# Giving solo projections four PSUM banks in turn in a two-layer hybrid trunk, and moving the norm's broadcast rows

## The chip, the cores and the metric

The kernel runs on one core of a Trainium2 chip. The metric is device microseconds of one execution, the median of several runs. A profile of one execution gives the busy times and waits of the engines: TensorE (PE, matmuls; PEld is its weight load), VectorE (DVE), ScalarE (ACT), GpSimd (POOL) and SyncE (SP, which issues the DMAs).

## The reference

Two layers act on 512 latent tokens `x` and 256 context tokens `y` of width 1024. Each layer norms the tokens, projects them, runs three branches (retention RET, neighbourhood attention NA, grouped-query attention GQA), and merges them under sigmoid gates:

```
hx = rms_norm(x, norm_w) * (1.0 + scale_x) + shift_x
rq, rk, rv, rg, nq, nk, nv, ng, gq, gk, gv, gg, mg = split_cols(hx @ w_in)
...
m = (g_ret * (ret_o @ w_ret_o) + g_na * (na_o @ w_na_o) + g_gqa * (gqa_o @ w_gqa_o))
x = x + gate_x * (m @ w_out)
```

Layer 1 updates `x` alone; a last `rms_norm` gives the output.

## The kernel before

Tokens lie in the free dimension, 768 in layer 0 (512 latent, 256 context), and 512 for most of layer 1. Every fp32 product is made of three fp32r matmuls (`mm3`, lines 278 to 280: high times high, high times low, low times high), so each weight block is split into `whi` (ACT, L262) and `wlo` (POOL, L264). One projection of a 128-wide column block over 512 tokens is a group of 24 matmuls into one PSUM bank, then an "evacuation", in which ACT and DVE read that bank and write SBUF. A projection with tokens in the partitions (`g_proj_tok`, lines 310 to 312) is three groups of 48 matmuls of 256 columns.

PSUM has eight banks. `bank(tag)` hands out tiles from four rings: two tiles of `pj`, two of `s`, three of `pt`, one of `pv`. A tile of a ring may be written when the tile that last held the same bank has been read by all its readers, so in a ring of two a group waits for the evacuation of the group before the last. Projections use `pj`; attention scores, the context rows' outputs (L477), the transposes of the GQA values (`tr`, L784), and the norm's broadcast rows (`bcast_mm`, L387) use `s`.

PE's order is that of the program text, by hand: `run(units)` emits projections with nothing between them ("alone"), `window(steps, units)` mixes attention steps with projections. `defer(us, fn)` puts off a piece of work until the projections emitted since have a given cost, and it then lands between two matmuls of whatever group is running. The orders of DVE and ACT are set by a list scheduler when the program is built, and then fixed.

Places that the text below speaks of:
- After the start phase (which holds four banks for `u_q(0)` and `u_k(0)` of NA at once: the latter's context part in `pj`, its latent part in `pv`, both parts of `u_q(0)` in `s`), `runs(na.u_v(0))` follows: three groups of L310.
- The GQA opening: `runs(gqa.u_k(), gqa.u_v(), gqa.u_q(0))`. The evacuation of `u_v` copies to `sg` (ACT, L779), and its transposes `tr` come 1.5 us of projections later, four for the latent part, two for the context part; each is read by one `gv` cast on ACT (L788) and one `gv` subtraction on DVE (L789). The keys meanwhile go through a long DVE chain that ends in `gk` (`k_fin`, L767 to L770).
- The retention heads: `run(u_qk(h,"q"), u_qk(h,"k"), ...)` before each head's window, evacuated by `ql` and `kl` (L974) on DVE.
- `finish`: the merges of the last branch, the output projection `g_out`, and `norm_part`, whose broadcast row is L387.

Of the kernel before, what the change touches and what calls it, by code (L numbers as in the profile page):

```python
# [39 lines left out]
def trunk_kernel(ctx: ExitStack, tc: tile.TileContext, xt, wcol, wv, adaw, wbr, wout, nabias, vecs,  # L40
# [3 lines left out]
    def tap(name, ap, where):  # L44
        if taps and name in taps:
            nc.sync.dma_start(out=taps[name][where], in_=ap)
# [12 lines left out]
    def bank(tag):  # L59
        return pp.tile([128, 512], F32, tag=tag, name=tag, bufs=PSB[tag])  # L60
# [3 lines left out]

    mm = nc.tensor.matmul
    env = {}


    clock = [0.0]
# [9 lines left out]
    def due(force=False):  # L79
        while waiting:  # L80
            w = min(waiting, key=lambda x: x[0])
            if not force and w[0] > clock[0]:
                return
            waiting.remove(w)
            w[2]()
# [19 lines left out]
            return c  # L105

    def run(units):
        for u in units:
            while u.step() is not None:
                pass  # L110

    NEED = 1.0
    def window(steps, units, lead=0.0, keep=0.0):
# [31 lines left out]
        if not keep:  # L145
            run(units)
# [121 lines left out]
    def getw(src):  # L268
        while len(ready) < 2 and stream:
            _load()  # L270
        s, parts = ready.pop(0)
        assert s is src, "weight stream order"
        while len(ready) < 1 and stream:
            _load()
        return parts

    def mm3(ps, sh, sl, mh, ml, start, stop):
        mm(ps, lhsT=sh, rhs=mh, start=start, stop=False)  # L278
        mm(ps, lhsT=sh, rhs=ml, start=False, stop=False)  # L279
        mm(ps, lhsT=sl, rhs=mh, start=False, stop=stop)  # L280
# [4 lines left out]
    def wk(parts, k, nk=4, width=128):  # L285
        hi, lo = parts[k // nk]
        c = slice((k % nk) * width, (k % nk) * width + width)
        return hi[:, c], lo[:, c]

    def g_proj(w, groups, evac):  # L290
        for o, n in groups:
            ps = bank("pj")
            for k in range(KT):
                sh, sl = wk(w, k)
                mh, ml = hx[k]
                mm3(ps[:, :n], sh, sl, mh[:, o:o + n], ml[:, o:o + n], k == 0, k == KT - 1)
                if k == KT - 1:
                    evac(ps[:, :n], o, n)
                yield 3 * n * NS

    def g_proj_tok(wa, wb, evac):
        for tp in range(3):
            ps = bank("pj")
            for i in range(2):
                tok = slice((2 * tp + i) * 128, (2 * tp + i) * 128 + 128)
                for k in range(KT):
                    hi, lo = wk(wa if k < 4 else wb, k % 4, 2, 256)
                    sh, sl = hx[k]
                    o = ps[:, i * 256:i * 256 + 256]
                    mm(o, lhsT=sh[:, tok], rhs=hi, start=(k == 0), stop=False)  # L310
                    mm(o, lhsT=sh[:, tok], rhs=lo, start=False, stop=False)  # L311
                    mm(o, lhsT=sl[:, tok], rhs=hi, start=False, stop=(k == KT - 1))  # L312
                    if i == 1 and k == KT - 1:
                        evac(ps, tp)
                    yield 3 * 256 * NS
# [4 lines left out]
    def u_proj(src, groups, evac):  # L320
        return Unit(sum(n for _, n in groups) * 24 * NS, [src], lambda ws: g_proj(ws[0], groups, evac), evac)
# [46 lines left out]
    def sumsq(acc, x, first, c, npool, bufs=2):  # L368
        n = c.stop - c.start
        if first:  # L370
            nc.scalar.activation(acc[:, c], x[:, c], AF.Square)
        else:
            sq = npool.tile([128, n], F32, tag="sq", name="sq", bufs=bufs)
            nc.scalar.activation(sq, x[:, c], AF.Square)
            nc.vector.tensor_tensor(acc[:, c], acc[:, c], sq, op=ALU.add)

    def stat_mm(acc, o, n):
        ss = bank("pt")
        for i in range(n // 128):
            mm(ss[:, i:i + 1], lhsT=acc[:, o + 128 * i:o + 128 * i + 128], rhs=ones, start=True, stop=True)  # L380
        return ss

    def bcast_mm(r, o, n, tag="s"):
        bc = bank(tag)
        for i in range(n // 128):
            tb = o // 128 + i
            mm(bc[:, 128 * i:128 * i + 128], lhsT=r[:, tb:tb + 1].to_broadcast([128, 128]), rhs=ident,  # L387
               start=True, stop=True)
        return bc
# [687 lines left out]
    def u_merge(l, b, d, g, m, getpool):  # L1077
        gq = G_ALL if l == 0 else G_LAT
        nq = NT if l == 0 else NX
        src = [ap_wcol[l][CT_MG + 8 * b + d]]  # L1080
        if d % 2 == 0:
            src.append(ap_wbr[l][b][d // 2])

        def gen(ws):
            if d % 2 == 0:
                wbr_now[0] = ws[1]
            t = getpool().tile([128, nq], F32, tag="mt", name="mt", bufs=1)

            def ev(ps, o, n):
                nc.scalar.activation(t[:, o:o + n], ps, AF.Tanh, scale=0.5)  # L1090
            yield from g_proj(ws[0], gq, ev)
            hi, lo = wbr_now[0][d % 2]
            if len(g) < 4:
                due(True)
            for o, n in gq:
                ps = bank("pj")
                for k in range(4):
                    c = slice(k * 128, k * 128 + 128)
                    gh, gl = g[k]
                    mm3(ps[:, :n], hi[:, c], lo[:, c], gh[:, o:o + n], gl[:, o:o + n], k == 0, k == 3)  # L1100
                    if k == 3:
                        c = slice(o, o + n)
                        if b == BR_NA:
                            nc.vector.scalar_tensor_tensor(m[d][:, c], t[:, c], 1.0, ps[:, :n], op0=ALU.add, op1=ALU.mult)
                        else:
                            nc.vector.scalar_tensor_tensor(t[:, c], t[:, c], 1.0, ps[:, :n], op0=ALU.add, op1=ALU.mult)  # L1106
                            nc.vector.tensor_tensor(m[d][:, c], m[d][:, c], t[:, c], op=ALU.add)
                    yield 3 * n * NS
        return Unit(nq * 36 * NS, src, gen)

    wbr_now = [None]
# [141 lines left out]
    def finish(l, m, mtp):  # L1253
# [27 lines left out]
        def g_out(half, o, n):  # L1281
            for d in range(KT):
                w = getw(ap_wout[l][half][d])
                xo = op.tile([128, 512], F32, tag="xo", name="xo", bufs=2)
                nc.sync.dma_start(out=xo[:, :n], in_=xsrc[:, d * st + o:d * st + o + n])
                ps = bank("pj")
                for k in range(KT):
                    sh, sl = wk(w, k)
                    mh, ml = mhl[k]
                    mm3(ps[:, :n], sh, sl, mh[:, o:o + n], ml[:, o:o + n], k == 0, k == KT - 1)  # L1290
                    if k == KT - 1:
                        s = 1 if o >= NX else 0
                        with tc.high_priority(HP):
                            nc.vector.scalar_tensor_tensor(xn[d][:, o:o + n], ps[:, :n], cG[l][:, d, s:s + 1], xo[:, :n],
                                                           op0=ALU.mult, op1=ALU.add)
                            sumsq(accs["t"], xn[d], d == 0, slice(o, o + n), op)
                        if l == 0 and o == 0:
                            nc.sync.dma_start(out=env["xsave"][:, d * NX:(d + 1) * NX], in_=xn[d][:, :NX])
                        tap(f"x{l}", xn[d][:, o:o + n], (d, slice(None), slice(o, o + n)))
                    yield 3 * n * NS  # L1300
# [6 lines left out]
        def norm_part(o, n, use, go, w1=3.0, w2=4.0):  # L1307

            r = cp.tile([128, 6], F32, tag="rstd", name="rstd", bufs=2)

            def one():
                ss = stat_mm(accs["t"], o, n)
                nb = n // 128
                rsqrt(r[:, o // 128:o // 128 + nb], ss[:, :nb], nb, 1.0 / D, EPS)
                go(w2, two)

            def two():
                bc = bcast_mm(r, o, n)
                for k in range(KT):
                    use(k, bc[:, :n], o, n)  # L1320
            go(w1, one)
# [10 lines left out]
        def hx_part(k, bcv, o, n):  # L1332
            make_hx(1, k, xn[k], bcv, o, n, npool)
        use = hx_part if l == 0 else out_part
        parts = ((0, 512), (512, 256)) if l == 0 else ((0, 256), (256, 256))
        if l == 0:
            new_hx()
        for half, (o, n) in enumerate(parts):
# [9 lines left out]
            else:  # L1348
                due(True)
                norm_part(o, n, use, lambda wait, fn: fn())  # L1350
        env["lo_dve"] = False
        cm.__exit__(None, None, None)
        mtp["cm"].__exit__(None, None, None)
        env["gcm"].__exit__(None, None, None)
# [129 lines left out]
```

## Time and profile before

| | |
|---|---|
| median of 3 runs | 1745.47 us (1740.78 to 1746.36) |
| profiled execution | 1744.02 us |
| its span, first to last instruction | 1742.2 us |
| mean granted TensorE clock | 0.993 |
| PE busy | 1665.9 us (96%) |
| DVE busy | 1056.7 us (61%) |
| ACT, POOL busy | 796.8 us (46%), 556.4 us (32%) |

PE's busy time is the sum of modelled matmul spans and touches 96% of the span; the other engines are well below. A row of a timeline gives start, duration, engine, line, operation, output and inputs, shapes, the count of equal instructions in a row, and in brackets the idle time of that engine just before and what ended it.

### The profile page before, as it was taken

How to read it: one execution, taken by the hardware profiler on the slowest of the kernel's cores; microseconds unless marked ns; L12 is line 12 of the kernel's file. 1: busy time of each engine (PE TensorE's matmuls, PEld its weight loads, DVE VectorE, ACT ScalarE, POOL GpSimd, SP SyncE). 2: the span in 40 equal slices, each digit the busy share in tenths (PEclk: the TensorE clock that was granted, in tenths of full speed). 3: DMA queues.
4: the chain of work that ended last, by engine and by line, in shares of the span. 5: the costliest groups of instructions: out<-in, count | busy, mean ns of one | idle time of the engine just before them, and what ended most of it. 6: DMA issues, size and time to landing. Idle time of an engine off the chain costs nothing. (4 is left out here: it accounts for less than half of the span.)

```text
span 1742.2 us, 26141 instructions
## 1 busy us (share of the span) xinstructions
PE 1665.9 (96%) x9940; PEld 1439.5 (83%) x9940; DVE 1056.7 (61%) x2201; ACT 796.8 (46%) x1570; POOL 556.4 (32%) x486
## 2 busy tenths in 40 slices
PE   6899999999999999999999999999999999999997
PEld 4778888888899889888887889877787897887786
DVE  6666567666654655565324766668677646555456
ACT  4455564555553443443223445654555544344342
POOL 1433332233233222322222343423333333243432
PEclk9999999999999999999999999999999999999998
DMA  8211111111111121214536521311111121122245
GB/s 317 80 51 56 58 49 49 37 49 37 37 60 49 49 61 37 63 50 157 203 133 206 171 97 47 99 49 61 49 58 52 60 73 61 61 76 70 91 136 160
DMA packets 43053, 146.38 MB, mean 84 GB/s; under 512 B 4912, under 2 KB 10160, under 8 KB 39856
## 3 DMA queue, kind: packets, MB, share of 16 engines
q1 hardware_dynamic: 42928, 144.72, 25.0%
q8 instruction: 78, 1.28, 0.3%
q14 instruction: 47, 0.39, 0.1%
HBM read 140.51 MB, written 4.19 MB: 83 GB/s over the span
## 5 line engine op out<-in xcount | busy, mean ns | idle before, releaser
L264 POOL TENSOR_TENSOR wlo<-raw,whi 128x512 fp32r<-128x512 f32 x345 | 457.3, 1330 | 972.3 <-ACT whi L262 923.6
L278 PE MATMUL pj<-hxh,whi 128*128 128x512 f32 (+1 forms) x1448 | 527.7, 364 | 9.8 <-DVE ql L974 3.9
L279 PE MATMUL pj<-hxl,whi 128*128 128x512 f32 (+1 forms) x1448 | 510.3, 352 | 1.1 <-DVE hxl L404 1.1
L280 PE MATMUL pj<-hxh,wlo 128*128 128x512 f32 (+1 forms) x1448 | 509.7, 352 | 0.0
L262 ACT CAST whi<-raw 128x512 fp32r<-128x512 f32 x376 | 231.4, 618 | 293.2 <-PE pj L279 214.8
L278 PEld LDWEIGHTS pj<-hxh,whi 128*128 128x128 f32 x1448 | 274.2, 189 | 43.1 <-DVE ql L974 5.8
L280 PEld LDWEIGHTS pj<-hxh,wlo 128*128 128x128 f32 x1448 | 273.9, 189 | 39.0
L279 PEld LDWEIGHTS pj<-hxl,whi 128*128 128x128 f32 x1448 | 274.9, 190 | 28.1 <-DVE hxl L404 2.2
L439 DVE TENSOR_TENSOR pl<-pt,ph 128x512 fp32r<-128x512 f32 (+2 forms) x208 | 126.7, 625 | 52.9 <-ACT ph L438 50.7
L278 PE MATMUL pj<-gat,whi 128*128 128x512 f32 (+1 forms) x416 | 144.6, 348 | 2.6 <-ACT gat L917 2.0
L279 PE MATMUL pj<-gat,whi 128*128 128x512 f32 (+1 forms) x416 | 142.4, 342 | 0.6 <-DVE gat L1271 0.3
L280 PE MATMUL pj<-gat,wlo 128*128 128x512 f32 (+1 forms) x416 | 142.0, 341 | 0.0
L438 ACT CAST ph<-pt 128x512 fp32r<-128x512 f32 (+2 forms) x208 | 107.6, 533 | 69.4 <-PE pt L624 29.4
L310 PE MATMUL pj<-whi,hxh 128*128 128x256 f32 x384 | 110.5, 288 | 3.1 <-DVE kz L427 2.3
L312 PE MATMUL pj<-whi,hxl 128*128 128x256 f32 x384 | 109.4, 285 | 0.0
L311 PE MATMUL pj<-wlo,hxh 128*128 128x256 f32 x384 | 109.4, 285 | 0.0
L278 PEld LDWEIGHTS pj<-gat,whi 128*128 128x128 f32 x416 | 79.2, 190 | 11.9 <-ACT gat L917 2.5
L862 ACT ACTIVATE p<-p,nm,rq 128x768 f32<-128x768 f32 x64 | 65.4, 1024 | 46.7 <-DVE nm L860 46.1
L280 PEld LDWEIGHTS pj<-gat,wlo 128*128 128x128 f32 x416 | 79.0, 190 | 9.4
L279 PEld LDWEIGHTS pj<-gat,whi 128*128 128x128 f32 x416 | 79.1, 190 | 8.9 <-DVE gat L1271 0.5
L853 DVE TENSOR_SCALAR_CACHE_REDUCE p<-s 128x384 f32<-128x384 f32 x128 | 69.0, 554 | 28.0 <-PE s L852 26.7
L1106 DVE SCALAR_TENSOR_TENSOR mt<-mt,pj 128x512 f32<-128x512 f32 (+1 forms) x48 | 28.6, 596 | 91.9 <-PE pj L280 91.3
(265 smaller groups left out, 2957.6 us busy)
## 6 DMA issues: line engine op xcount, KB each, us to landing
raw<-in_wcol_dram SPq DMA_DIRECT2D x116, 512.0 KB, 3.5
araw<-in_adaw_dram SPq DMA_DIRECT2D x24, 1024.0 KB, 6.4
raw<-in_wout_dram SPq DMA_DIRECT2D x32, 512.0 KB, 3.5
raw<-in_wbr_dram SPq DMA_DIRECT2D x24, 512.0 KB, 3.5
raw<-in_wv_dram SPq DMA_DIRECT2D x16, 512.0 KB, 3.5
bias<-in_nabias_dram SPq DMA_DIRECT2D x16, 384.0 KB, 3.1
x<-in_xt_dram SPq DMA_DIRECT2D x8, 384.0 KB, 6.0
xo<-in_xt_dram SPq DMA_DIRECT2D x8, 256.0 KB, 3.7
```

Of the source, the lines that this page charges most:

```text
L262: nc.scalar.copy(hi, raw[:, c])
L264: lo_eng.tensor_tensor(lo, raw[:, c], f(hi), op=ALU.subtract)
L278: mm(ps, lhsT=sh, rhs=mh, start=start, stop=False)
L279: mm(ps, lhsT=sh, rhs=ml, start=False, stop=False)
L280: mm(ps, lhsT=sl, rhs=mh, start=False, stop=stop)
L310: mm(o, lhsT=sh[:, tok], rhs=hi, start=(k == 0), stop=False)
L311: mm(o, lhsT=sh[:, tok], rhs=lo, start=False, stop=False)
L312: mm(o, lhsT=sl[:, tok], rhs=hi, start=False, stop=(k == KT - 1))
L438: nc.scalar.copy(ph[:, :n], pt[:, :n])
L439: nc.vector.tensor_tensor(pl[:, :n], pt[:, :n], f(ph[:, :n]), op=ALU.subtract)
L853: nc.vector.tensor_scalar(P[:, jj, kk], s[:, :384], 1.0, -3.0e38, op0=ALU.mult, op1=ALU.max, accum_out=mx[:, i:i + 1])
L862: nc.scalar.activation(P[:, a], P[:, a], AF.Exp, bias=nm[:, a:a + 1], scale=rqe[:, 2 * hf + a:2 * hf + a + 1], accum_out=sm[:, a:a + 1])
```

## The change

A function `pbank()` hands out the bank of a projection group. While the flag `alone` is set (inside `run`, and in `finish` from the output projection on) it gives `s` and `pj` in turn; otherwise `pj`. The turn goes on over the whole program: it is toggled at every projection group, alone or not. The broadcast rows in `finish` go to `pv` (first part) and `pt` (second part) in place of `s`. The numbers of banks per ring stay as they are.

```diff
+    turn = [0]
+    def pbank():
+        turn[0] ^= 1
+        return bank("s" if env.get("alone") and turn[0] else "pj")
...
     def run(units):
+        env["alone"] = True
         for u in units:
             while u.step() is not None:
                 pass
+        env["alone"] = False
...
     def g_proj(w, groups, evac):
         for o, n in groups:
-            ps = bank("pj")
+            ps = pbank()
...
     def g_proj_tok(wa, wb, evac):
         for tp in range(3):
-            ps = bank("pj")
+            ps = pbank()
...
             for o, n in gq:
-                ps = bank("pj")
+                ps = pbank()
...
-                ps = bank("pj")
+                ps = pbank()
                 for k in range(KT):
                     sh, sl = wk(w, k)
                     mh, ml = mhl[k]
...
             def two():
-                bc = bcast_mm(r, o, n)
+                bc = bcast_mm(r, o, n, "pv" if o == 0 else "pt")
...
         use = hx_part if l == 0 else out_part
+        env["alone"] = True
...
-        env["lo_dve"] = False
+        env["lo_dve"] = env["alone"] = False
```

PE's order of work, and those of POOL and SP, are the same; banks differ, and with them what PE waits for. DVE and ACT differ in a few places only. Lines of the change stand 6 to 9 lower down than those of before; the numbers after tile names are the same in both programs.

The first place is PE at the first group of `u_v(0)` in layer 0 (tile 621), just after the start phase. Before:

```order
L278 MATMUL pj_263<-hxh_179,whi_147 128x256
L279 MATMUL pj_263<-hxl_180,whi_147 128x256
L280 MATMUL pj_263<-hxh_179,wlo_148 128x256
L310 MATMUL pj_621<-whi_252,hxh_165 128x256
L311 MATMUL pj_621<-wlo_253,hxh_165 128x256 [waits Pool_49]
L312 MATMUL pj_621<-whi_252,hxl_166 128x256
```

Now:

```order
L286 MATMUL pj_263<-hxh_179,whi_147 128x256
L287 MATMUL pj_263<-hxl_180,whi_147 128x256
L288 MATMUL pj_263<-hxh_179,wlo_148 128x256
L318 MATMUL s_621<-whi_252,hxh_165 128x256 [waits DVE_49,PE_49]
L319 MATMUL s_621<-wlo_253,hxh_165 128x256 [waits Pool_49]
L320 MATMUL s_621<-whi_252,hxl_166 128x256
```

Tile 621 moved from the free `pj` bank to the first `s` bank, which holds the latent part of `u_q(0)` (tile 260), and waits for DVE. The second group of `u_v(0)` takes the free `pj` bank and waits for nothing, the third the other `s` bank.

The second place is PE in the GQA opening of layer 0: the first group of `u_q(0)` (tile 2969), with the second transposes `tr` (tile 2976) inside it. Before:

```order
L278 MATMUL pj_2969<-hxh_167,whi_2856 128x512
L279 MATMUL pj_2969<-hxl_168,whi_2856 128x512
L280 MATMUL pj_2969<-hxh_167,wlo_2857 128x512
L784 MATMUL s_2976<-ident_90,sg_2918 128x128 [waits Activation_49]
L784 MATMUL s_2976<-ident_90,sg_2918 128x128
```

Now:

```order
L286 MATMUL s_2969<-hxh_167,whi_2856 128x512
L287 MATMUL s_2969<-hxl_168,whi_2856 128x512
L288 MATMUL s_2969<-hxh_167,wlo_2857 128x512
L792 MATMUL s_2976<-ident_90,sg_2918 128x128 [waits DVE_49]
L792 MATMUL s_2976<-ident_90,sg_2918 128x128
```

The projection now stands in the `s` ring between the first transposes (tile 2930) and the second (2976), so 2976 falls on the bank of 2930 and waits for DVE to have read it; before it waited for ACT's copy `sg` alone. Layer 1 reads the same with tiles 12457 and 12503. On DVE, at the same place, before (`gk` are the halves of the keys):

```order
L789 TENSOR_TENSOR gv_2760<-s_2930,gv_2760 128x2x64
L789 TENSOR_TENSOR gv_2760<-s_2976,gv_2760 128x2x64
L768 TENSOR_TENSOR gk20_2758<-kr_2796,gk10_2756 64x768
L769 CAST gk10_2756<-gk10_2756 64x768
L770 CAST gk20_2758<-gk20_2758 64x768
L768 TENSOR_TENSOR gk21_2759<-kr_2796,gk11_2757 64x768
L769 CAST gk11_2757<-gk11_2757 64x768
L770 CAST gk21_2759<-gk21_2759 64x768
L789 TENSOR_TENSOR gv_2760<-s_2930,gv_2760 128x2x64
L789 TENSOR_TENSOR gv_2760<-s_2976,gv_2760 128x2x64
```

Now:

```order
L797 TENSOR_TENSOR gv_2760<-s_2930,gv_2760 128x2x64
L776 TENSOR_TENSOR gk20_2758<-kr_2796,gk10_2756 64x768
L777 CAST gk10_2756<-gk10_2756 64x768
L778 CAST gk20_2758<-gk20_2758 64x768
L776 TENSOR_TENSOR gk21_2759<-kr_2796,gk11_2757 64x768
L777 CAST gk11_2757<-gk11_2757 64x768
L778 CAST gk21_2759<-gk21_2759 64x768
L797 TENSOR_TENSOR gv_2760<-s_2930,gv_2760 128x2x64 x3
L797 TENSOR_TENSOR gv_2760<-s_2976,gv_2760 128x2x64 x2
```

Three of the four readers of tile 2930 stand behind the six instructions on the keys. On ACT, in layer 1, the casts of the weights that stood ahead of and among the `gk` and `gv` casts stand behind them: before,

```order
L788 CAST gv_12287<-s_12503 128x2x64
L262 CAST whi_12539<-raw_12533 128x512
L767 CAST gk10_12283<-kr_12323 64x768
L767 CAST gk11_12284<-kr_12323 64x768
L788 CAST gv_12287<-s_12457 128x2x64
L788 CAST gv_12287<-s_12503 128x2x64
L262 CAST whi_12545<-raw_12543 128x512
```

and now

```order
L775 CAST gk10_12283<-kr_12323 64x768
L775 CAST gk11_12284<-kr_12323 64x768
L796 CAST gv_12287<-s_12457 128x2x64 x3
L796 CAST gv_12287<-s_12503 128x2x64 x2
L270 CAST whi_12539<-raw_12533 128x512
L270 CAST whi_12545<-raw_12543 128x512
```

The weights of the next projection are now cast only after the readers of 12503, and so POOL's `wlo` of them too.

The third place is PE in a retention head of layer 1, where the latent part of `u_qk(1,"k")` (tile 15165) gives way to its context part (15194); the query before them is tile 15126 in `pj`, before as now. Before:

```order
L278 MATMUL pj_15165<-hxh_9584,whi_15122 128x512
L279 MATMUL pj_15165<-hxl_9585,whi_15122 128x512
L280 MATMUL pj_15165<-hxh_9584,wlo_15123 128x512
L278 MATMUL pj_15194<-hxh_9570,whi_15118 128x256 [waits DVE_49]
L279 MATMUL pj_15194<-hxl_9571,whi_15118 128x256
```

Now:

```order
L286 MATMUL s_15165<-hxh_9584,whi_15122 128x512
L287 MATMUL s_15165<-hxl_9585,whi_15122 128x512
L288 MATMUL s_15165<-hxh_9584,wlo_15123 128x512
L286 MATMUL pj_15194<-hxh_9570,whi_15118 128x256 [waits DVE_49]
L287 MATMUL pj_15194<-hxl_9571,whi_15118 128x256
```

Before, 15194 stood on the bank of the query 15126; now 15165 has left the ring, so 15194 stands on the bank of the merge group ahead of the query, and the next `pj` group on that of the query. In layer 0 the second and third head begin with `pj` again, the fourth head and `finish` with `s`.

## Rows read from the trace of the kernel before

**Rows 1.** The page: busy us, share of the span and instructions of each engine.

```profile
PE 1665.9 (96%) x9940; PEld 1439.5 (83%) x9940; DVE 1056.7 (61%) x2201; ACT 796.8 (46%) x1570; POOL 556.4 (32%) x486
```

**Rows 2.** Waits of PE: waiter, releaser: us in total, times, longest.

```profile
PE pj L278 <- DVE ql L974: 3.9, 6, 0.9
PE pj L310 <- DVE kz L427: 2.3, 1, 2.3
PE pj L278 <- DVE mt L1106: 2.0, 4, 0.5
...
PE pj L278 <- DVE kl L974: 1.2, 2, 0.8
...
PE pj L310 <- DVE kl L974: 0.8, 1, 0.8
PE pj L278 <- DVE kz L427: 0.7, 1, 0.7
```

**Rows 3.** Timeline of PE, second retention head of layer 1.

```profile
1462.28 0.38 PE L278 MATMUL pj<-hxh,whi 128*128 128x256 f32 x1 [0.92 <-DVE ql L974]
...
1466.18 0.50 PE L278 MATMUL pj<-hxh,whi 128*128 128x512 f32 x1 [0.78 <-DVE kl L974]
...
1468.36 0.39 PE L278 MATMUL s<-qh,kh 128*128 128x512 f32 x1
```

**Rows 4.** Timeline of DVE, same place.

```profile
1465.45 0.68 DVE L974 SCALAR_TENSOR_TENSOR kl<-pj,kh 128x512 fp32r<-128x512 f32 x1
```

**Rows 5.** Timeline of PE, first and second group of u_v(0), layer 0.

```profile
55.61 0.28 PE L310 MATMUL pj<-whi,hxh 128*128 128x256 f32 x1
...
63.86 0.36 PE L310 MATMUL pj<-whi,hxh 128*128 128x256 f32 x1 [2.34 <-DVE kz L427]
```

**Rows 6.** Timeline of DVE, same place.

```profile
60.17 1.04 DVE L427 SCALAR_TENSOR_TENSOR q<-s,q 64x512 fp32r<-64x512 f32 x2
```

**Rows 7.** Timeline of PE, second transposes of the GQA opening, layer 0.

```profile
269.90 0.44 PE L784 MATMUL s<-ident,sg 128*128 128x128 f32 x2 [0.75 <-ACT sg L779]
```

**Rows 8.** Timeline of DVE, same place.

```profile
272.48 0.68 DVE L707 TENSOR_TENSOR kr<-kr,sh 128x512 f32<-128x512 f32 x1
...
274.06 0.95 DVE L768 TENSOR_TENSOR gk<-kr,gk 64x768 fp32r<-64x768 f32 x1 [0.50 <-ACT gk L767]
...
278.14 0.49 DVE L789 TENSOR_TENSOR gv<-s,gv 128x128 fp32r<-128x128 f32 x2
```

**Rows 9.** Timeline of ACT, same place.

```profile
274.91 0.43 ACT L788 CAST gv<-s 128x128 fp32r<-128x128 f32 x2
```

**Rows 10.** Timeline of PE, GQA opening of layer 1.

```profile
1194.02 0.44 PE L784 MATMUL s<-ident,sg 128*128 128x128 f32 x2 [0.74 <-ACT sg L779]
...
1201.75 0.66 PE L725 MATMUL pt<-ident,gsq 128*128 128x128 f32 x4 [1.14 <-ACT gsq L719]
...
1212.19 0.41 PE L851 MATMUL s<-gk,q 128*128 128x384 f32 x1 [0.91 <-DVE q L427]
```

**Rows 11.** Timeline of DVE, same place.

```profile
1196.60 1.77 DVE L707 TENSOR_TENSOR kr<-kr,sh 128x512 f32<-128x512 f32 x1
...
1201.31 2.05 DVE L768 TENSOR_TENSOR gk<-kr,gk 64x768 fp32r<-64x768 f32 x1
...
1204.46 0.49 DVE L789 TENSOR_TENSOR gv<-s,gv 128x128 fp32r<-128x128 f32 x2
```

**Rows 12.** Timeline of POOL, same place.

```profile
1201.28 1.27 POOL L264 TENSOR_TENSOR wlo<-raw,whi 128x512 fp32r<-128x512 f32 x1 [3.45 <-ACT whi L262]
```

**Rows 13.** Timeline of PE at the end of the last retention window.

```profile
1617.51 0.51 PE L278 MATMUL pj<-gat,whi 128*128 128x512 f32 x1 [2.04 <-ACT gat L917]
```

**Rows 14.** Stretches: length; busy us (instructions) of PE, PEld, DVE, ACT, POOL; granted clock; DMA.

```profile
64.00:68.00 4.00, 4.00 (x35) 4.00 (x36) 0.88 (x3) 0.37 (x1) 0.00 (x0) 1.00 0.02 4
...
1618.80:1622.20 3.40, 3.40 (x10) 2.62 (x9) 2.47 (x3) 1.24 (x2) 1.27 (x1) 0.51 0.10 14
1622.20:1626.00 3.80, 3.80 (x18) 3.16 (x17) 0.52 (x1) 0.73 (x2) 1.29 (x1) 0.99 0.34 125
```

## The prediction

> **What bounds the kernel now.** The page comes first: PE is busy for 96% of the span and DVE for 61% [rows 1]. A change that moves no matmul can only give back, or add, time in which PE stands still, so the view to read next is the one of PE's waits. There the waits that two `pj` banks make are those of a projection (L278, L310) for a DVE evacuation: `ql` 3.9 us in six waits, `kl` 1.2 and 0.8 in three, `mt` 2.0 in four, `kz` 2.3 and 0.7 in one each, 10.9 us in all [rows 2]. That is about the most the change can win, 0.6% of the span. One instance shows the pattern: in the second head of layer 1 the context part of the key projection waits 0.92 us for `ql`, and the next group 0.78 for `kl` [rows 3]. Third, since a wait can move as well as vanish, I followed each tile of the changed order to the tile that held its bank before, and looked up in the timelines of DVE and ACT when that one is read out. Three tiles come out late, and they decide the sign; at the other changed places the bank has been read out before PE comes.
>
> **What the change gives back.** All six waits for `ql` go, since the tile in front of them left the `pj` ring; so do the three for `kl`. Of the four for `mt` two stay: the second and third head of layer 0 still begin on `pj` behind the merges; two go, 1.0 us. The `kz` wait before the first NA window of layer 1 (0.7) goes. Sum 3.9 + 2.0 + 1.0 + 0.7 = 7.6 us in twelve waits [rows 2]. The idle time understates each: a matmul of 512 columns is shown for 0.39 us [rows 3] while their starts are 0.21 us apart (18 in 3.80 us [rows 14]), so a wait costs about 0.17 more than its bracket, 2.0 us over twelve: 9.6. Some comes back as a wait for data. In layer 1's second head the scores stand at 1468.36 [rows 3] and would come two waits and overlaps, 2.0 us, earlier, at 1466.3; the key they need is done at 1465.45 + 0.68 = 1466.13 [rows 4], so almost all is kept there. I take off 0.8 for narrower places, and keep **8.8 us** (bounds 7.0 and 9.6).
>
> **What it adds: `u_v(0)` of layer 0.** Its first group starts at 55.61 in a free `pj` bank and its second at 63.86 after 2.34 us of waiting [rows 5], so a group takes 63.86 - 55.61 - 2.34 = 5.9 us at most. Now the first group stands on the bank of `u_q(0)`, whose last reader is the first of the pair `q` that starts at 60.17 [rows 6]. The pair's 1.04 us covers 512 and 256 columns, so the first part ends near 60.8 and PE starts near 61.0. The second group, which now has a free bank, then starts near 66.7 in place of 63.86: **+2.9 us**. The 2.3 us for `kz` in rows 2 is thereby replaced, not won.
>
> **The GQA opening, layer 0.** This is the dearest term. The second transposes stand at 269.90 [rows 7] and now need the bank of the first, whose four `gv` readers on DVE are in the new order one ahead of the key instructions and three behind. The keys still start at 274.06, when ACT's cast lets them [rows 8], and end where the `gv` pair now stands, at 278.14 [rows 8]. Two `gv` take 0.49, so three end near 278.9; ACT's casts for them are done long before, at 274.91 and after [rows 9]. PE starts near 279.0 rather than 269.90: **+9.1 us**. Nothing covers it: behind the transposes in PE's queue stand the rest of `u_q(0)`, the first merge and the window, and the queries that the window's scores need come out of that very projection. The key chain doesn't wait for PE.
>
> **The GQA opening, layer 1.** The same transposes stand at 1194.02 [rows 10], the `gv` pair at 1204.46 [rows 11]; three `gv` later it would be 1205.2, a stall of 11.3 us. But two steps of that chain are long here: `kr` 1.77 and one `gk` 2.05 [rows 11], where layer 0 took 0.68 and 0.95 [rows 8]. The long `gk` starts beside a POOL `wlo` of 1.27 us at 1201.28 [rows 12]. In the new ACT order the weight casts that feed such `wlo` stand behind the `gv` casts, so POOL has nothing to do there; if both steps shrink to layer 0's size the chain ends 2.1 to 2.2 us sooner. I take 9.2 (bounds 9.1 and 11.3), because the order removes the overlap. On SBUF — State Buffer, section Who interferes with whom, the Trainium skill says that a VectorE instruction with two SBUF inputs contends with a GpSimd instruction that reads SBUF. The trace agrees, 2.05 against 0.95 us; were it not the cause, the time would be 2.1 us more. Two data waits later in this stage, 1.14 for `gsq` and 0.91 for `q` [rows 10], exist because ACT and DVE are still busy with the keys; after the stall they aren't, so these go, with their overlaps -2.3. Net **+6.9 us**.
>
> **The clock.** After a wait of 2.04 us at 1617.51 [rows 13] PE ran 3.4 us at a granted clock of 0.51, the level of 1.2 GHz: 10 matmuls there, against 18 in the 3.80 us that follow at 0.99 [rows 14], so 1.3 us were lost. After the 2.34 us of rows 5 it stayed at 1.00 [rows 14]. Three stalls of 5 to 9 us should each cost such a stretch: 3 x 1.3 = **+3.9 us** (bounds 0, as after rows 5, and 10.2, where each restart has two such stretches at half pace, 3.4 us lost). The Trainium skill's TensorE: Matmul & The Clock Gate, Part 1, says that the array drops from 2.4 to 1.2 GHz after idling and comes back after sustained activity; by that rule all three stalls pay, as I have it, and the trace's one stretch above agrees.
>
> **The broadcast rows.** Four matmul groups change bank. At each, PE waits for `rstd` on DVE, not for a bank, and nothing else is in `pv` or late in `pt` there: 0.
>
> **Sum.** 2.9 + 9.1 + 6.9 + 3.9 - 8.8 = +14.0 us on the profiled execution's 1744.02: **1758 us**, or 0.8% slower. That execution stands 1.5 us below the median of the three runs, which differ by 5.6 among themselves; a change within 0.3% (5.2 us) can hardly be told from none here.
>
> **Rivals.** (1) The stalls come, the clock holds: 1754 us, 0.12. For it speaks the stretch after rows 5, against it that after rows 13. (2) The stalls come dear: layer 1 keeps its long steps (+2.1), the half-clock stretches are longer or two each: 1764 to 1768 us, 0.13. (3) The other side: the wait for the first transposes' bank costs nothing, because the `gv` readers finish before PE arrives. This decides at one place, DVE in the GQA opening: if the three `gv` were done before 269.90, 9.1 + 9.2 us and their clock would fall away, leaving 2.9 + 1.3 - 8.8 = -4.6 (there the 2.3 of relief has no cause), 1739 us, faster by 0.3%. Against it: their order is fixed, behind instructions that can't start before 274.06; it needs a bank assignment other than the one I read. 0.07. (4) The change does nothing that can be measured, because PE's waits for `ql` and `kl` come back one for one as waits for data and the stalls are about half what I have, being met by PE's slack elsewhere: 1749, 0.06. PE's 96% leave little slack.
>
> The likeliest, 1758, has 0.62 and its own range 1755 to 1762. The range for 8 in 10 reaches to (1) and into (2): 1750 to 1766, with the spread of the runs. Slower by over 0.3% takes the likeliest, (1) and (2): 0.87; same 0.07, faster 0.06.
>
> **What the next profile should show.** Right: PE's waits name a transpose into `s` (now L792) for `gv` with some 18 us in two; a wait of about 5 us for `q` ahead of L318; no wait of a projection for `ql` or `kl`, and two for `mt`; the granted clock at half after each of the three. Wrong if the transposes wait for ACT alone, or if the retention heads keep their pairs of waits. The sum is off by the clock if the stretches after the stalls show 1.00.

## The result, and the profile after

The changed kernel took 1764.68 us (median of four runs, 1764.03 to 1766.47) against 1745.91 for the kernel before beside it: ratio 1.0119, 95% interval 1.0107 to 1.0131, some 20.8 us (the two medians alone differ by 18.8). The forecast was 1758, or 0.8% slower, with 1755 to 1762 as the range of its likeliest case and 1750 to 1766 as the wide one: sign and mechanism came out, the size did not. The profiled execution took 1766.47 us, the longest of the four, span 1764.7, mean granted clock 0.981.

Of PE's waits in the changed kernel these bear on the argument (lines 262 to 1294 of before stand 8 lower here); the columns are those of [rows 2].

```profile
PE s L792 <- DVE gv L797: 21.1, 2, 10.5
...
PE s L318 <- DVE q L435: 5.2, 1, 5.2
...
PE pv L395 <- DVE rstd L219: 3.2, 1, 3.2
...
PE pj L286 <- DVE mt L1114: 1.0, 2, 0.5
...
PE s L319 <- POOL wlo L272: 0.7, 1, 0.7
```

All waits for `ql`, `kl` and `kz` of [rows 2] are gone and two of the four for `mt` are left, as forecast. In their place stand one wait of 5.2 us and two of 10.5. The timeline of PE shows where, first at `u_v(0)` (before: [rows 5]), then at the second transposes of the two layers (before: [rows 7, 10]).

```profile
60.89 0.55 PE L318 MATMUL s<-whi,hxh 128*128 128x256 f32 x1 [5.19 <-DVE q L435]
...
286.07 0.69 PE L792 MATMUL s<-ident,sg 128*128 128x128 f32 x2 [10.54 <-DVE gv L797]
286.41 0.78 PE L286 MATMUL s<-hxh,whi 128*128 128x512 f32 x1
286.99 0.63 PE L287 MATMUL s<-hxl,whi 128*128 128x512 f32 x1
...
1217.58 0.69 PE L792 MATMUL s<-ident,sg 128*128 128x128 f32 x2 [10.54 <-DVE gv L797]
```

The matmuls behind the stall show 0.63 us where the same form shows 0.39 at full clock. What PE waits for stands on DVE (answers to [rows 8]):

```profile
279.42 0.28 DVE L797 TENSOR_TENSOR gv<-s,gv 128x128 fp32r<-128x128 f32 x1
280.40 0.95 DVE L776 TENSOR_TENSOR gk<-kr,gk 64x768 fp32r<-64x768 f32 x1 [0.70 <-ACT gk L775]
...
283.90 0.55 DVE L778 CAST gk<-gk 64x768 fp32r<-64x768 f32 x1
284.48 0.29 DVE L797 TENSOR_TENSOR gv<-s,gv 128x128 fp32r<-128x128 f32 x1
285.10 0.29 DVE L797 TENSOR_TENSOR gv<-s,gv 128x128 fp32r<-128x128 f32 x1 [0.33 <-ACT gv L796]
285.73 0.29 DVE L797 TENSOR_TENSOR gv<-s,gv 128x128 fp32r<-128x128 f32 x1 [0.33 <-ACT gv L796]
```

and on ACT (answers to [rows 9]):

```profile
281.24 0.27 ACT L796 CAST gv<-s 128x128 fp32r<-128x128 f32 x1
284.80 0.27 ACT L796 CAST gv<-s 128x128 fp32r<-128x128 f32 x1 [3.30 <-DVE gv L797]
285.43 0.27 ACT L796 CAST gv<-s 128x128 fp32r<-128x128 f32 x1 [0.36 <-DVE gv L797]
```

One `gv` stands ahead of the keys and three behind, as read from the order. But the three don't run back to back: each cast on ACT waits for the subtraction before it on DVE, and each subtraction for its cast, 0.62 us a pair where the forecast had 0.25.

The stretches behind the stalls, with the busy time of PE alone, then the granted clock (before: [rows 14]):

```profile
60.00:64.00 4.00, 3.11 (x14) 0.50 0.01 2
64.00:68.00 4.00, 4.00 (x29) 0.79 0.00 0
94.00:98.00 4.00, 2.69 (x8) 0.80 0.42 131
98.00:102.00 4.00, 4.00 (x22) 0.77 0.00 0
286.00:292.00 6.00, 5.93 (x17) 0.58 0.00 0
1217.00:1223.00 6.00, 5.42 (x14) 0.51 0.00 0
```

0.50 is the 1.2 GHz level. It holds for 4.6 to 5.2 us of PE's work behind each of the three stalls, and for 3.4 us more at 96 us, where PE's waits are those of before (0.74 and 0.99 us) and the clock of the kernel before was at 1.00.

How much later the same matmul starts after the change, followed through the two profiled executions, gives the ledger:

| Place (start before, us) | Step | Later by, us |
|---|---|---|
| 63.86, second group of `u_v(0)` | wait for `q` 2.85 net, half clock 2.1 | 5.0 |
| 93.63 | half clock at 96 us | 6.4 |
| 269.90, second transposes, layer 0 | wait for `gv` 9.8 | 16.2 |
| 276.78 | half clock 2.3 | 18.4 |
| 1035.98 | retention of layer 0 and the norm, -5.1 | 13.3 |
| 1194.02, second transposes, layer 1 | wait for `gv` 9.9, small drifts 0.4 | 23.6 |
| 1196.83 | half clock 2.4 | 25.9 |
| 1201.75 | wait for `gsq` gone, -1.3 | 24.7 |
| 1244.54 | waits for `q` and `p` shorter, new wait for `m`, together -0.2; longer half clock 1.0 | 25.5 |
| 1577.20 | retention of layer 1, -5.4 | 20.1 |
| end | last norm: `rstd` and half clock 2.3 | 22.5 |

### The profile page after: what moved, and what is told of

It reads as the page before. It is cut to its first block, busy times and chain, and to the rows that moved or that the text cites. A ratio compares the mean times of both kernels' runs of the same rounds, so it can differ in the third digit from the quotient of the medians.

```text
span 1764.7 us, 26125 instructions
## 1 busy us (share of the span) xinstructions
PE 1672.6 (95%) x9940; PEld 1448.3 (82%) x9940; DVE 1059.3 (60%) x2201; ACT 797.8 (45%) x1570; POOL 556.9 (32%) x486
## 5 line engine op out<-in xcount | busy, mean ns | idle before, releaser
L286 PE MATMUL pj<-hxh,whi 128*128 128x512 f32 (+1 forms) x1136 | 407.5, 359 | 1.1 <-DVE mt L1114 1.0
L288 PE MATMUL pj<-hxh,wlo 128*128 128x512 f32 (+1 forms) x1136 | 392.6, 346 | 0.0
L287 PE MATMUL pj<-hxl,whi 128*128 128x512 f32 (+1 forms) x1136 | 392.6, 346 | 0.0
L286 PE MATMUL s<-hxh,whi 128*128 128x512 f32 (+1 forms) x328 | 127.5, 389 | 1.8 <-ACT hxh L411 1.8
L287 PE MATMUL s<-hxl,whi 128*128 128x512 f32 (+1 forms) x328 | 125.6, 383 | 2.9 <-DVE hxl L412 2.9
L288 PE MATMUL s<-hxh,wlo 128*128 128x512 f32 (+1 forms) x328 | 124.4, 379 | 0.0
L286 PE MATMUL pj<-gat,whi 128*128 128x512 f32 (+1 forms) x312 | 109.5, 351 | 2.0 <-ACT gat L925 2.0
L287 PE MATMUL pj<-gat,whi 128*128 128x512 f32 (+1 forms) x312 | 107.3, 344 | 0.2 <-DVE gat L926 0.2
L286 PEld LDWEIGHTS s<-hxh,whi 128*128 128x128 f32 x328 | 63.5, 194 | 18.6 <-ACT hxh L411 3.4
L287 PEld LDWEIGHTS s<-hxl,whi 128*128 128x128 f32 x328 | 63.5, 194 | 15.9 <-DVE hxl L412 5.6
L286 PEld LDWEIGHTS pj<-gat,whi 128*128 128x128 f32 x312 | 59.9, 192 | 8.8 <-ACT gat L925 2.5
```

## Experiments

**The dear place undone.** The opening of GQA takes its own two banks in both layers again, the rest stays as changed.

```
-    def run(units):
-        env["alone"] = True
+    def run(units, alone=True):
+        env["alone"] = alone
...
-        runs(gqa.u_k(), gqa.u_v(), gqa.u_q(0))
+        plan.append(("run", [gqa.u_k(), gqa.u_v(), gqa.u_q(0)], False))
```

> The changed kernel with one thing undone: in the opening of GQA, in both layers, the three projections take only their own two banks again. Theory A (the two stalls of 10.5 us before the second transposes, and the half-clock stretches behind them, carry the loss): the changed kernel's trace grew by 9.8 + 2.2 us and 9.9 + 2.4 us against the one before at these two places, and gained 2.1 us of later waits there, so 1764.7 - 24.3 + 2.1 = about 1742 us, a little under the kernel before, and no wait of a transpose for gv. Rival B (the stalls cost what was forecast, and the rest of the overshoot lies elsewhere, in the finish, the broadcast rows or a clock that is low for another reason): 1764.7 - 18 + 2 = about 1748 us, above the kernel before. Rival C (the stalls are covered by slack later in the stage): over 1755 us.

Measured: 1741.01 us, ratio to before 0.9988 (0.9979 to 0.9997). Theory A, within a microsecond: no transpose waits for `gv`, and the change without this place is no longer a loss. The place costs 1.19 + 0.12 = 1.31%, 22.9 us.

**The second place undone too.**

```
-            runs(na.u_v(0))
+            plan.append(("run", [na.u_v(0)], False))
```

> The kernel of the first run of this set, with the first NA value projection of layer 0 on its own two banks as well. Theory A: its 5.2-us wait for q and the slow clock behind it go, 6.35 us by the traces at 93 us, so 1742 - 6.4 = about 1736 us, 0.6% under the kernel before: what is left of the change is the twelve waits given back, 8.8 us forecast. Rival B (the twelve waits come back as waits for data, so that the gain of the retention heads is small): 1742 to 1746 us, no different from the kernel before.

Measured: 1735.78 us, 0.9953 (0.9938 to 0.9968). Theory A again: `u_v(0)` cost 0.35%, 6.1 us (5.2 by the medians), and what is left of the change gains 0.47%, 8.2 us, beside the 8.8 forecast. The wait for `kz` of [rows 5] is back, and no projection waits for `ql` or `kl`; here and in the run before, the first merge of layer 0 waits 1.0 us for a `gv` reader.

```profile
PE pj L318 <- DVE kz L435: 2.3, 1, 2.3
```

**Each loss alone, on the kernel before.** First only the opening of GQA in four banks, then only `u_v(0)`; the diff gives the kernel before `pbank` and a flag that is set for these runs alone.

```
-        runs(gqa.u_k(), gqa.u_v(), gqa.u_q(0))
+        plan.append(("run", [gqa.u_k(), gqa.u_v(), gqa.u_q(0)], True))
```

> The kernel before with one part of the change alone: only the opening of GQA takes the four banks in turn, the broadcast rows stay where they were. Theory A: 9.8 + 2.2 us in layer 0 and 9.9 + 2.4 - 2.1 in layer 1, so before + 22 = about 1768 us, slower than the whole change, since nothing is given back. Rival B (the clock costs 1.3 us at each stall): before + 9.8 + 1.3 + 9.9 + 1.3 - 2.1 = about 1766. Rival C (the stalls make the loss only together with the other banks' use): under 1755 us.

Measured: 1766.04 us, 1.0121 (1.0108 to 1.0134), 21.1 us: between A's 22.2 and B's 20.6, nearer to B by the time, and the interval of 2.3 us each way parts it from neither. C falls.

```
-            runs(na.u_v(0))
+            plan.append(("run", [na.u_v(0)], True))
```

> The kernel before with one part of the change alone: only the first NA value projection of layer 0 takes the four banks in turn. Theory A: a wait of 5.2 us for q in place of 2.3 us for kz, +2.9 us, and a half-clock stretch behind it, +2.1, in all 5.0 us, to 6.4 where the clock falls once more at 93 us: 1751 to 1752 us. Rival B (the clock holds after it): 1749 us. Rival C (the wait is covered by a later one): 1746 us.

Measured: 1749.09 us, 1.0021 (1.0012 to 1.0030), 3.7 us with 2.1 to 5.2 as the interval: nearer to B's 2.9, though A's 5.0 isn't excluded. Its twelve runs spread from 1744.61 to 1751.65, and the profiled one is the fastest: it has the 5.19-us wait, and yet the clock was back at 1.00 by 64 us and stayed there at 96.

```profile
60.00:64.00 4.00, 3.07 (x15) 0.57 0.01 2
64.00:68.00 4.00, 4.00 (x35) 1.00 0.00 0
```

So the wait gives 2.9 us in both profiled executions, and the clock's part differs: 1.3 us here, 2.1 and another 1.4 at 96 us in the changed kernel. The other eleven runs have no trace; their mean granted clock falls from 0.994 in the fastest to 0.990 in the slowest.

**The readers first.** The banks stay as changed; the four `gv` readers get the scheduler's higher priority on ACT and DVE.

```
+                        with tc.high_priority(SQ):
-                        nc.scalar.copy(v[:, :, 0:64], src)
-                        nc.vector.tensor_tensor(v[:, :, 64:128], src, f(v[:, :, 0:64]), op=ALU.subtract)
+                            nc.scalar.copy(v[:, :, 0:64], src)
+                            nc.vector.tensor_tensor(v[:, :, 64:128], src, f(v[:, :, 0:64]), op=ALU.subtract)
```

> The changed kernel with the banks as they are, and only the order of two engines changed: the gv readers of the first transposes stand ahead of the key chain on ACT and DVE. Theory A (the second transposes wait because the readers of the first stand behind the keys): both 10.5-us waits fall to under 2 us and the slow clock behind them goes, so as in the kernel that keeps two banks there, about 1742 us, and up to 1745 since the keys come some 1.2 us (four gv) later. Rival B (bank sharing itself is the cost, whatever the order of the readers): over 1755 us.

Measured: 1739.69 us, 0.9972 (0.9961 to 0.9983), 1.5% under the changed kernel with the same banks. Theory A, and a little under its 1742: it isn't the shared bank that costs, it is the place of its readers in the queues. Two short waits are left:

```profile
276.19 0.44 PE L792 MATMUL s<-ident,sg 128*128 128x128 f32 x2 [1.95 <-DVE gv L798]
...
1197.85 0.44 PE L792 MATMUL s<-ident,sg 128*128 128x128 f32 x2 [1.94 <-DVE gv L798]
```

**The clock by itself.** Extra matmuls that nobody reads, in a bank of their own, fill the three stalls; all else is as changed.

```
+    def fill(count):
+        ps = bank("pv")
+        for i in range(count):
+            mm(ps, hx[0][0][:, 0:128], hx[1][0][:, 0:512], start=True, stop=True)
...
+        if not env.get("filled"):
+            env["filled"] = True
+            fill(22)
         for tp in range(3):
...
+                    if o > 0:
+                        fill(46)
                     pt = bank("s")
```

> The changed kernel with extra matmuls whose result nobody reads, 46 ahead of each late pair of transposes and 22 ahead of the first NA value projection of layer 0, 9.8 and 4.7 us at 0.213 us each: they fill the three stalls and leave the waits' ends where they are. What is measured is the cost of the clock by itself. Theory A (the half-clock stretches behind the three stalls and at 96 us cost 2.1 + 1.4 + 2.2 + 2.4 us in the profiled execution, and they come because PE stood still): 1764.7 - 8.1 = about 1757 us, with the granted clock at 1.00 there. Rival B (they cost 1.3 us each, as forecast): about 1761 us. Rival C (the clock falls whatever PE does there): 1765 us, half clock at the same places.

Measured: 1766.47 us, 1.0118, which says nothing yet. At `u_v(0)` the extra matmuls needed `pv`, which `kz` held, as this kernel's waits of PE show:

```profile
PE pv L301 <- DVE kz L443: 5.7, 1, 5.7
```

They came after the stall and made it longer. With that group in `pt`, which is free there:

```
-            fill(22)
+            fill(22, "pt")
```

> The changed kernel with the same extra matmuls in the three stalls, whose result nobody reads, those ahead of the first NA value projection now in a bank that is free there (in the earlier filled kernel they waited 5.7 us for theirs and so came behind the stall, which made that place 4.8 us later; at the two places in GQA they filled the stall and the granted clock stayed at 1.00). Theory A (the slow clock behind the three stalls and at 96 us costs 8.1 us in the profiled execution): 1764.7 - 8.1 = about 1757 us. Rival B (1.3 us at each of the three): about 1761 us. Rival C (no gain, since the slow stretches come again further on): 1764 to 1766 us.

Measured: 1758.48 us, 1.0077 (1.0063 to 1.0091), 6.2 us under the changed kernel by the medians and 7.3 by the ratios. That lies between A and B, nearer to A; C falls. The stalls are there in full (the same matmul is 9.8 us later at each of the two transposes), the clock is not lowered:

```profile
272.04 10.59 PE L301 MATMUL pv<-hxh 128*128 128x512 f32 x46
282.79 0.44 PE L802 MATMUL s<-ident,sg 128*128 128x128 f32 x2 [0.16 <-DVE gv L807]
```

```profile
60.00:64.00 4.00, 3.76 (x28) 1.00 0.01 3
64.00:68.00 4.00, 4.00 (x36) 1.00 0.03 6
94.00:98.00 4.00, 4.00 (x23) 1.00 0.20 79
286.00:292.00 6.00, 6.00 (x42) 1.00 0.08 5
```

42 matmuls in the 6 us of 286 to 292 stand beside 17 in the changed kernel, though this kernel is at another point of the program there. The stretch at 96 us is gone with the others. The 6 to 7 us are a net figure: by the two traces this kernel also lacks the half clock near 1264 us, 2.4 us, and has waits for `pl` and `ph` of 0.3 to 0.9 us, some 3 us in all with what hangs on them, that the changed kernel hasn't.

**The order in which the readers are written.** ACT's casts of all blocks first, then DVE's subtractions.

```
                         nc.scalar.copy(v[:, :, 0:64], src)
+                    for i in range(n // 128):
+                        v = self.V[:, o // 128 + i]
+                        src = pt[:, 128 * i:128 * i + 128].rearrange("p (h d) -> p h d", h=2)
                         nc.vector.tensor_tensor(v[:, :, 64:128], src, f(v[:, :, 0:64]), op=ALU.subtract)
```

> The changed kernel with the readers of a transposed bank written in another order: ACT's casts of all its blocks first, then DVE's subtractions, where the kernel writes them in pairs, block by block. In the changed kernel a cast and a subtraction take turns behind the key chain, 0.62 us a pair. Theory A (the turns come from the order in which they are written): the casts are done ahead, the subtractions run back to back at 0.25 us each, the waits fall from 10.5 to about 9.5 us each, and the time by 2 us to about 1763. Rival B (the two engines can't read one bank freely): pairs of 0.62 us again and 1764.7 us.

Measured: 1747.43 us, 1.0015 (1.0006 to 1.0023), 17.3 under the changed kernel: both theories were far off. The casts no longer wait for DVE, as A had it, and the subtractions run together; but since the casts are early, the scheduler now puts all four subtractions ahead of the keys on DVE, and the waits fall to 4.9 us each, not 9.5. (The profile names ACT's `gk`, which runs at that time; the last subtraction ends at 280.00 and PE starts at 280.14.)

```profile
272.10 0.43 ACT L796 CAST gv<-s 128x128 fp32r<-128x128 f32 x2 [0.43 <-PE s L792]
272.94 0.45 ACT L796 CAST gv<-s 128x128 fp32r<-128x128 f32 x2
```

```profile
279.13 0.87 DVE L800 TENSOR_TENSOR gv<-s,gv 128x128 fp32r<-128x128 f32 x4
280.10 0.95 DVE L776 TENSOR_TENSOR gk<-kr,gk 64x768 fp32r<-64x768 f32 x1
```

```profile
280.14 0.66 PE L792 MATMUL s<-ident,sg 128*128 128x128 f32 x2 [4.90 <-ACT gk L775]
```

The waits account for 2 x 5.6 = 11.2 of the 17.3 us, and the shorter half clock behind them for 1.3 (1.8 and 1.6 us where the changed kernel lost 2.3 and 2.4). In the two profiled executions, whose spans are 1764.7 and 1745.5 us, the rest is 0.5 us at `u_v(0)` and half-clock stretches near 1264, 1640 and 1736 us that the changed kernel has and this one hasn't. Why they go was not tried.

**Every run on the scores' bank first.** On the kernel with both losses undone, the turn is set back at the start of each run.

```
         env["alone"] = alone
+        turn[0] = 0
```

> The kernel in which both the opening of GQA and the first NA value projection keep two banks, with the turn set back at the start of each run, so that each run's first group stands on the scores' bank. Theory A: the two waits for mt that the change left go too, 2 x (0.5 + 0.17) = 1.3 us, so 1736 - 1.3 = about 1734.5 us, hardly to be told from 1736, and no wait of a projection for mt at a run's start in the trace. Rival B (another run now begins on a score bank that is still being read): a new wait of over 1 us and 1737 us or more.

Measured: 1739.55 us, 0.9974 (0.9964 to 0.9983), 3.8 us slower than without. The two waits for `mt` do go, as theory A has it, but rival B decides: the first merge of layer 1 now begins on the bank of the second transposes, and waits for their `gv` readers behind the keys. (A strict turn would give it the bank of the first transposes; the last of those readers ends 0.9 us after the merge has begun, so the ring gave out the bank that came free sooner.)

```profile
1203.84 0.77 PE L287 MATMUL s<-hxh,whi 128*128 128x512 f32 x1 [6.50 <-DVE gv L798]
```

**The broadcast rows alone.** On the kernel before.

```
-                bc = bcast_mm(r, o, n)
+                bc = bcast_mm(r, o, n, "pv" if o == 0 else "pt")
```

> The kernel before with the broadcast rows of the norms alone moved to the other banks, no projection changed. Theory A (they wait for rstd and not for a bank): no difference, 1744 to 1746 us. Rival B (the longer wait for rstd in the changed kernel's last norm, 3.2 us against 2.0, comes from the rows' banks): a wait for rstd of 3 us again, and 1746 to 1747 us.

Measured: 1743.29 us, 0.9991 (0.9982 to 1.0000). Theory A; the wait of the rows in `pv` is 1.9 us here, so the 3.2 of the changed kernel doesn't come from the rows' bank.

**Two ways of mending, together.** First the readers first and two banks for `u_v(0)`; then two banks at both places and the readers first as well. Both combine edits shown above, with no other.

> The changed kernel with both of its losses mended in their own way: the gv readers ahead of the key chain, with four banks in the opening of GQA, and two banks for the first NA value projection of layer 0. Theory A (the two losses add up): the kernel with the readers first, 1739.7, less the 6.1 us by which two banks in that projection differed, about 1733.5 us, 0.7% under the kernel before. Rival B (the 2-us waits for gv that are left, with their slow clock, cost what the four banks give there): 1736 us or more.

Measured: 1735.43 us, 0.9952 (0.9940 to 0.9964).

> Two banks in the opening of GQA and in the first NA value projection, as in the best kernel so far, and the gv readers ahead of the key chain as well. Theory A (with two banks there nothing of PE waits for gv, so their order gains nothing, and the keys come 1 us later without anyone waiting): 1735 to 1737 us, no difference. Rival B (the later keys delay the first GQA window): 1738 us or more, with a wait of the window's scores for gk.

Measured: 1735.65 us, 0.9951 (0.9939 to 0.9963). For the second kernel theory A holds in the time, though the first window's scores now wait 2.0 us for `m` where they waited 0.8. The first lies between its A (1733.5) and B (1736), so whether four banks in GQA are worth anything beside readers that come first stays open. Three kernels stand at 1735.4 to 1735.8, and nothing tells them apart: each gains about 0.5% on the kernel before and 1.6% on the change.

## Why the prediction was right in sign and short in size

The step of the prediction that failed is the price of the clock, "3 x 1.3 = +3.9 us": the trace shows 8.2 in its place. The steps in order:

**What the change gives back** (8.8 us forecast): right. The kernel that keeps this part and none of the losses gains 8.2 us, and the waits that go are those named.

**`u_v(0)`** (+2.9): right as a wait, 2.85 us net. With the clock the place cost 6.1 us in the changed kernel and 3.7 alone on the kernel before, which the intervals don't part.

**The GQA opening** (+9.1 and +9.2): the mechanism was right, and so was each time of the key chain. In the changed kernel the first subtraction of the keys starts at 280.40; less the 6.35 us by which all is later there this is 274.05, beside 274.06 in [rows 8]. In layer 1 the overlap with POOL went, as forecast: `kr` took 0.68 us and the second `gk` 0.95 (before: 1.77 and 2.05 in [rows 11]).

```profile
1213.94 0.95 DVE L776 TENSOR_TENSOR gk<-kr,gk 64x768 fp32r<-64x768 f32 x1
```

The waits added 9.8 and 9.9 us. What was misread here is "three end near 278.9", with ACT's casts "done long before": the last reader ended 0.8 us later, because casts and subtractions wait for each other in turn. The trace of the kernel before has it already, outside the rows that were read; of the four casts of the first transposes two stand later than [rows 9], and the earlier of them waits for a `gv` on DVE:

```profile
278.47 0.27 ACT L788 CAST gv<-s 128x128 fp32r<-128x128 f32 x1 [0.18 <-DVE gv L789]
```

Taking turns costs only 0.7 us of each wait. But in the kernel with the casts first, where it is gone, the scheduler puts the subtractions ahead of the keys, and the same banks cost 17 us less.

**The relief in layer 1** (-2.3): the waits for `gsq` and `q` did go (-2.1), but the scores then waited 0.8 us for `m` in place of `q`, so 1.4 us were kept with a shorter wait for `p`. The wait for `m` is one for a bank: the scores stand on one of the `s` ring that a merge, alone before the window, now holds. So the sentence that at all other places the bank has been read out before PE comes was wrong at this place.

**The clock** (3 x 1.3 = +3.9): this is the term that was mis-sized, and the main reason why the time lies outside the likeliest case. The one price was a single stretch of 3.4 us behind a 2-us wait [rows 13, 14]. Behind the three longer stalls PE ran 4.6 to 5.2 us at half pace, 2.1, 2.3 and 2.4 us lost, and 1.4 at 96 us, where the prediction had no stall: 8.2 by the trace, and 6 to 7 net by the run in which extra matmuls fill the stalls. The upper bound that the prediction kept (10.2) held that, and its rival of dear stalls (1764 to 1768, chance 0.13) is what came in time and by the longer stretches, though without the long steps of layer 1. (The chances it sums up as 0.07 for the same and 0.06 for faster stand the other way round in its rivals (3) and (4).)

Together, in the profiled executions and beside the forecast: waits for `gv` +1.4, relief +0.9, clock behind the three stalls +2.9 and at 96 us +1.4, a longer half-clock stretch at 1264 us +1.0, small drifts +0.4, the last norm +2.3, gains -1.7 (5.1 + 5.4 in the ledger against 8.8) make +8.6, and 22.5 - 14.0 = 8.5 were measured.

The last norm's part, a `rstd` wait 1.2 us longer and a half-clock stretch behind it, wasn't in the prediction at all. The broadcast rows alone don't cause it. The wait goes with the four banks of the output projection: it is 2.4 to 3.4 us in the ten profiled kernels that have them and 1.9 to 2.0 in the four that haven't. In the trace the DVE chain that makes `rstd` stands behind a `wlo`, and that behind ACT's `whi`, which waits for the DMA of the weights and starts 21.0 us later than before, where PE is only 19.8 later. First the kernel before, then the changed one:

```profile
1708.36 0.62 ACT L262 CAST whi<-raw 128x512 fp32r<-128x512 f32 x1 [2.31 <-DMA raw<-in_wout_dram]
```

```profile
1729.39 0.62 ACT L270 CAST whi<-raw 128x512 fp32r<-128x512 f32 x1 [2.88 <-DMA raw<-in_wout_dram]
```

Why the weights come no sooner was not tried.

## What to carry to other kernels

A tile that takes its turn in another ring waits for the last reader of the tile that stood there, so follow that reader to its place in its own engine's queue, and also to the other engine's instructions that it waits for. More banks are worth it where the borrowed bank is read out in time: the same rotation lost 1.2% with two places where it wasn't and won 0.5% without them, and with the readers put first the four banks of GQA lost nothing that could be measured. The Trainium skill's Perfetto Trace Analysis, section Matmul Optimizations, advises to see that all eight PSUM banks are used; the runs here agree for the retention heads and disagree for the two projections whose borrowed bank was read out late.

A stall of several microseconds costs again in the clock. Price it from more than one stretch, and keep the upper bound near the middle of the range when all the new stalls are longer than the one that was measured.

## What the hardware showed that was not expected

The clock answers the same wait in different ways. Seven of the profiled kernels have the 2.3-us wait for `kz` before the second group of `u_v(0)`, with PE's work in the same order up to there. In three the clock stayed at 1.00 from 64 to 68 us, just behind it (before: [rows 14], both losses undone, the rows alone), in four it fell (only GQA in four banks 0.60, each run on the scores' bank first 0.70, the two ways of mending 0.66 and 0.57). First the kernel with both losses undone, then the one with only GQA in four banks, then the one that starts each run on the scores' bank:

```profile
64.00:68.00 4.00, 3.88 (x32) 1.00 0.02 6
```

```profile
64.00:68.00 4.00, 3.78 (x20) 0.60 0.02 6
```

```profile
64.00:68.00 4.00, 3.78 (x23) 0.70 0.03 6
```

The Trainium skill's TensorE: Matmul & The Clock Gate, Part 1, says that the number of slow matmuls with which a kernel starts varies between its runs. These rows show the like behind a wait in the middle of a kernel, each in one execution of its program. The times fit it but don't prove it: the twelve runs of the kernel with `u_v(0)` alone spread by 7.0 us, and the seventeen of the kernel before, without its stall, by 6.4. So part of what a stall costs seems to be settled anew in each execution, and a single profile prices it badly.
